# Expert layers of a transformer: TensorE's order fixed to blocks of full and half columns, the norm's output transposed back instead of added by identity matmuls

## The chip, the cores and the metric

The kernel runs on one core of a Trainium2 chip. The metric is the device time of one execution in microseconds (us). TensorE does the matmuls and transposes, VectorE (DVE), ScalarE (ACT) and GpSimd (POOL) work elementwise, and SyncE (SP) issues the DMAs that bring the weights from HBM. [...]

## The reference, cut to what matters

256 tokens of 1024 features go through a block with two feed-forward parts and a mixer, then through two further layers, each with a mixer of its own, a norm, a mixture of experts and a gated embedding, and a second norm. The change touches the expert part of these two layers:

```python
x = layer_norm(DEEPNORM_ALPHA * x + mix, ln_mix_g[i], ln_mix_b[i])
ple = (p[i] @ ple_w_proj[i]) * jax.nn.sigmoid(x @ ple_w_gate[i])
ffn = grouped_moe(x, router_w, router_bias, moe_w1[i], moe_w3[i], moe_w2[i])
x = layer_norm(DEEPNORM_ALPHA * x + ffn + ple, ln_ffn_g[i], ln_ffn_b[i])

def grouped_moe(x, router_w, router_bias, w1, w3, w2):   # 16 experts, two per token
    ...                                                  # gates: (tokens, 16)
    h = jax.nn.silu(jnp.einsum('td,edf->etf', xt, w1)) * jnp.einsum('td,edf->etf', xt, w3)
    h = h * gates.T[:, :, None].astype(h.dtype)          # w1, w3: 1024 x 512 per expert
    y = jnp.einsum('etf,efd->td', h, w2)                 # w2: 512 x 1024 per expert
```

## The kernel before

**Tiling.** `moe_layer` works on pairs of experts, p = 0 to 7. The router gives each expert up to 64 slots for its tokens. Three kinds of step follow for each pair. *Gather*: one-hot matrices `oh` pull the tokens' features (in two parts, `nh` and `nl`) into slots, `xgp<-oh,nh` and `xgp<-oh,nl`, 256 columns each, for two pairs at once: 32 matmuls at p = 0, 2 and 4 (and ahead of the loop). *Up* (`up`): `h1` and `h3` are 16 program matmuls each, with 64 slots as the stationary columns. Expert e=0 writes rows 0 to 63 of the PSUM tile and e=1 rows 64 to 127, so each matmul uses one half of the array's columns and the two experts alternate. *Down* (`down`): the product `es` of silu(h1) and h3 is transposed in four pieces (`hidden_T`, `ehT`, copied to `ehTs`), and 16 more half-column program matmuls give `ey`. These half-column operands are plain fp32, and the trace holds two records for each program matmul, so `h` shows 64 records a pair and `ey` 32.

**Combine.** `ey` is scaled and split into two fp32r parts `yh` (ScalarE) and `yl` (VectorE), and `combine` adds them into the tokens with eight full-column matmuls by the transposed one-hots `ohT` (made in `slots_T` from `ohTp`). For p = 0 to 2 they go to PSUM tiles `early` that VectorE adds into `x` (tile `acc`); from p = 3 (`last`) they accumulate in four PSUM banks `comb`. Two more things are added into `comb` by matmuls with the identity: 32 of `xTh` and `xTl`, the norm's output held transposed (128 features by 256 tokens, two parts), at the end of p = 3, and eight of `acch` and `accl`, the two parts of `x`, at the end of p = 6. The gate of the embedding, `gacc`, is 96 full-column matmuls during p = 1 to 3 and holds the same four banks before `comb`. The end of the layer reads `comb` for the norm's statistics (`bst`).

**The branch.** At p = 4 the kernel reads a flag (`ci`): if an expert got more than 64 tokens, the rest is computed by `overflow`. In the runs shown the branch jumps over it. Every engine has its own copy of the branch, L1400, and of the join behind it.

**What sets the order.** Python emits instructions in program order and a scheduler then orders each engine's list by dependences, priorities and its own cost figures. `after(i, j)` adds a pure order between two instructions. In the expert loop nothing but data, buffers and the branch fixes TensorE's order. The weights come through a ring of tiles of 512 KB (`Stream`, `W.next`); SP issues each load when the tile's last reader is done, in the fixed order of the list of loads. `mm` (L342) and `mm3` (L337) are the helpers that issue nearly all matmuls, so their lines, L343 and L338 to L340, name many different things in the profile; tiles' names tell them apart.

Of the kernel before, what the change touches and what calls it, by code (L numbers as in the profile page):

```python
# [15 lines left out]
P = 128  # L16
# [33 lines left out]
def transformer_kernel(ctx: ExitStack, tc: tile.TileContext, A, out, stop=None):  # L50
# [67 lines left out]
    def fb(ap):  # L118
        return ap.bitcast(F32)
# [211 lines left out]
    def split_to(hi, lo, src, scale=1.0):  # L331
# [2 lines left out]
            return V.tensor_tensor(lo, src, fb(hi), op=OP.subtract)  # L334
        return V.scalar_tensor_tensor(lo, src, scale, fb(hi), op0=OP.mult, op1=OP.subtract)  # L335

    def mm3(o, lh, ll, rh, rl, start, stop):  # L337
        PE.matmul(o, lh, rh, start=start, stop=False)  # L338
        PE.matmul(o, lh, rl, start=False, stop=False)  # L339
        PE.matmul(o, ll, rh, start=False, stop=stop)  # L340
# [746 lines left out]
    def layer_norm_T(x, before, row, eps, then=None):  # L1087

        qs, hi, lo = [[], []], [], []

        def allocate():
            hi.extend(H([4, T], F32R, "xTh") for _ in range(2))
            lo.extend(H([4, T], F32R, "xTl") for _ in range(2))

        def split(i):
            tk = slice(i * P, (i + 1) * P)
            for kk in range(2):
                split_to(hi[kk][:, :, tk], lo[kk][:, :, tk], qs[i][kk])

        def chunks():  # L1100
            return ([hi[k // 4][:, k % 4, :] for k in range(8)], [lo[k // 4][:, k % 4, :] for k in range(8)])

        def later():
            allocate()
            split(0)
            split(1)
            return chunks()
# [125 lines left out]
    def slots_T(oh, sc, p):  # L1233

        t_ = PT([T + NE], name="ohTp")
        for t in range(2):
            PE.transpose(t_[:, t * P:(t + 1) * P], fb(oh[p // 2])[:, t, p % 2 * P:(p % 2 + 1) * P], ident)  # L1237
# [30 lines left out]
    def moe_layer(i, x, before, row, eps, next_gains):  # L1268
# [75 lines left out]
        def hidden_T(s):  # L1344
            ht = PT([4, P], name="ehT")
            for f in range(4):
                PE.transpose(ht[:, f, :], s[:, f * P:(f + 1) * P], ident)  # L1347
            hT = Q([4, P], name="ehTs")
            S.copy(hT, ht)  # L1349
            return hT  # L1350

        def down(p, hT, sg):
            ys = [PT([512], name="ey") for _ in range(2)]
            for f in range(4):
                ws = [W.next() for _ in range(2)]
# [4 lines left out]
            y = [(Q([512], F32R, "yh"), Q([512], F32R, "yl")) for _ in range(2)]  # L1360
            for j in range(2):
                split_to(*y[j], ys[j], sg)
            return y

        def combine(p, y, o):

            skip = dict(skip_group_check=True) if p >= last else {}
            for t in range(2):
                o_ = o[:, t * P:(t + 1) * P]
                cs = [PT([512], name="early") for _ in range(2)] if p < last else comb[t]  # L1370
                for j in range(2):
                    mm(cs[j], o_, y[j][0], start=p <= last, stop=False, **skip)
                for j in range(2):
                    mm(cs[j], o_, y[j][1], start=False, stop=p < last or p == 7, **skip)
                    if p < last:
                        d = slice(j * 512, (j + 1) * 512)
                        if p == 0:
                            V.tensor_copy(x[t][:, d], cs[j])
                        else:
                            V.tensor_tensor(x[t][:, d], x[t][:, d], cs[j], op=OP.add)  # L1380

        last = len(PLE) - 3
        acc = [[PA([512], name="gacc") for _ in range(2)] for _ in range(2)]

        def gate(k):
            wh, wl = wsplit(G)
            for t in range(2):
                for j in range(2):
                    c = slice(j * 512, (j + 1) * 512)
                    tk = slice(t * P, (t + 1) * P)  # L1390
                    mm3(acc[t][j], xTh[k][:, tk], xTl[k][:, tk], wh[:, 0, c], wl[:, 0, c], k == 0, k == 7)

        h1, h3 = PT([512], name="h1"), PT([512], name="h3")
        up(0, h1)
        up(0, h3)
        s = hidden(h1, h3)
        for p in range(8):
            if p == 4:
                v = nc.values_load(ci[0:1, 0:1], min_val=0, max_val=T)
                with tc.If(v > CAP):  # L1400
                    overflow(i, x, nh, nl, late, row)
            if p < 7:
                h1 = PT([512], name="h1")
                up(p + 1, h1, (0, 1))
            hT = hidden_T(s)
            if p < 7:
                up(p + 1, h1, (2, 3))
            o, sg = slots_T(oh, sc, p)
            if p == 7:
                gains(*next_gains, W.loads[W.pos + 7])  # L1410
            y = down(p, hT, sg)
            if p == 0:
                xTh, xTl = xT()
            if p <= last:
                for k in range(*PLE[p + 1:p + 3]):
                    gate(k)
            if p == last:
                for t in range(2):
                    for j in range(2):
                        c = slice(j * 512, (j + 1) * 512)  # L1420
                        g = Q([512], name="pg")
                        S.activation(g, acc[t][j], AF.Sigmoid)
                        V.tensor_tensor(g, g, pro[t][:, c], op=OP.mult)
                        V.tensor_tensor(x[t][:, c], x[t][:, c], g, op=OP.add)
                comb = [[PA([512], name="comb") for _ in range(2)] for _ in range(2)]
            if p < 7:
                h3 = PT([512], name="h3")
                up(p + 1, h3)
                s = hidden(h1, h3)
                if p % 2 == 0 and p < 6:  # L1430
                    oh.append(onehot(rk, p // 2 + 1))
                    gather(p // 2 + 1, oh)
            if p == 0:

                x[:] = [H([D], name="acc") for _ in range(2)]
            combine(p, y, o)
            if p == last:
                for t in range(2):
# [5 lines left out]
            if p == 6:  # L1444
                for t in range(2):
                    xs = XH([D], F32R, "acch"), X([D], F32R, "accl")
                    split_to(*xs, x[t])
                    for part in xs:
                        for j in range(2):
                            mm(comb[t][j], identr, part[:, j * 512:(j + 1) * 512], start=False, stop=False,  # L1450
                               skip_group_check=True)
        return lambda t: comb[t]

    def overflow(i, x, nh, nl, late, row):
# [248 lines left out]
```

## Time and profile before

| | us |
|---|---|
| median of 3 executions (lowest to highest) | 1340.33 (1338.78 to 1343.26) |
| the profiled execution, its own time | 1343.85 |
| its span in the trace | 1342.2 |
| PE busy / DVE busy / ACT busy / POOL busy | 1281.4 / 600.3 / 514.1 / 266.2 |
| layer 0's experts: to the branch, round the branch, behind it | 145.59, 29.14, 86.13 |
| layer 1's experts: the same three, and the tail to the end | 144.49, 28.33, 86.20, 14.33 |

The span is the time from the first to the last instruction of the profiled execution; its own time also has what lies around it. A stage in the table is a stretch of the trace: "to the branch" starts with the first pair's `h`, "round the branch" starts where pair 4's last `h` ends, "behind it" ends with the last `ey`. In a row of the timeline, the first number is the start in us from the span's start, the second the length up to the end of the last instruction in the row, and `x8` means eight instructions of this kind in a row on that engine. Matmuls overlap in the pipeline, so the pace of TensorE is the distance from one start to the next, and not the length. [...] The DMA share counts the core's 16 DMA engines, and can come out a little over 1.

### The profile page before, as it was taken

To read this page: it belongs to the slowest core of one execution; us is meant where nothing else is said; L and a number is where in the kernel's file an instruction comes from. 1 tells how busy PE (TensorE), PEld (TensorE's weight loads), DVE (VectorE), ACT (ScalarE), POOL (GpSimd) and SP (SyncE) were. 2 spreads that over 40 slices of the span, in tenths; PEclk is the share of its full clock that TensorE was granted. 3 is DMA by queue.
4 is the path that set the end of the run, shared out by engine and by line. 5 is a ranking of instruction groups with operands and counts; after the bars stand their busy time and mean duration, and the time that the engine had idled before them with its cause. 6 is when DMAs were issued, how large, how long until landed. Compare 5 with 4: busy or idle time off the path is not lost. (4 is left out here: it accounts for less than half of the span.)

```text
span 1342.2 us, 19692 instructions
## 1 busy us (share of the span) xinstructions
PE 1281.4 (95%) x7758; PEld 913.1 (68%) x7758; DVE 600.3 (45%) x959; ACT 514.1 (38%) x774; POOL 266.2 (20%) x318
## 2 busy tenths in 40 slices
PE   8999999999998999989999999997999999999996
PEld 7999987877897999878444554334988635454432
DVE  6554458786665455586241221107555522121113
ACT  5444445575444544435221131104676421131110
POOL 4000010003699273240011020004021110220001
PEclk9999999999998999999989998997999999998998
DMA  9666656444453556559789999998535698999991
GB/s 341 219 186 187 189 158 203 128 156 142 150 180 126 157 174 197 187 174 336 275 317 370 394 342 342 385 382 285 186 109 193 236 383 319 381 344 357 366 402 38
DMA packets 175277, 335.41 MB, mean 250 GB/s; under 512 B 10338, under 2 KB 72306, under 8 KB 175171
## 3 DMA queue, kind: packets, MB, share of 16 engines
q1 hardware_dynamic: 173696, 330.34, 70.2%
q0 software_dynamic: 896, 2.98, 0.6%
q8 instruction: 66, 1.08, 0.3%
q10 hardware_dynamic: 578, 0.67, 0.2%
q14 instruction: 41, 0.33, 0.1%
HBM read 332.91 MB, written 1.05 MB: 249 GB/s over the span
## 5 line engine op out<-in xcount | busy, mean ns | idle before, releaser
L316 DVE TENSOR_TENSOR wlo<-w,whi 128x1024 fp32r<-128x1024 f32 x200 | 256.9, 1289 | 215.4 <-ACT whi L301 210.5
L301 ACT ACTIVATE whi<-w 128x1024 fp32r<-128x1024 f32 x234 | 246.4, 1059 | 268.4 <-PE hT L339 119.7
L343 PE MATMUL h<-w,xg 128*64 128x512 f32 x1024 | 254.4, 607 | 0.0
L338 PE MATMUL hT<-xTh,whi 128*128 128x256 f32 x704 | 201.7, 287 | 0.1
L339 PE MATMUL hT<-xTl,whi 128*128 128x256 f32 x704 | 201.1, 286 | 0.3 <-DVE xTl L334 0.2
L340 PE MATMUL hT<-xTh,wlo 128*128 128x256 f32 x704 | 200.5, 285 | 0.0
L343 PEld LDWEIGHTS h<-w,xg 128*64 128x64 f32 x1024 | 73.4, 139 | 137.8 <-issue 129.3
L339 PEld LDWEIGHTS hT<-xTl,whi 128*128 128x128 f32 x704 | 136.9, 195 | 1.4 <-DVE xTl L334 0.8
L338 PEld LDWEIGHTS hT<-xTh,whi 128*128 128x128 f32 x704 | 136.9, 194 | 1.3 <-ACT xTh L332 0.5
L340 PEld LDWEIGHTS hT<-xTh,wlo 128*128 128x128 f32 x704 | 136.7, 194 | 0.0
L343 PE MATMUL ey<-w,ehTs 128*64 128x512 f32 x512 | 115.1, 595 | 0.2
L316 POOL TENSOR_TENSOR wlo<-w,whi 128x1024 fp32r<-128x1024 f32 x16 | 38.0, 2399 | 242.6 <-ACT whi L301 242.6
L343 PEld LDWEIGHTS ey<-w,ehTs 128*64 128x64 f32 x512 | 38.2, 137 | 65.1 <-issue 60.0
L335 DVE SCALAR_TENSOR_TENSOR yl<-ey,sgate,yh 128x512 fp32r<-128x512 f32 x32 | 23.6, 749 | 124.2 <-ACT yh L332 123.4
L338 PE MATMUL tr<-xTh,whi 128*128 128x256 f32 x256 | 73.9, 289 | 0.4 <-ACT xTh L332 0.4
L339 PE MATMUL tr<-xTl,whi 128*128 128x256 f32 x256 | 73.2, 286 | 0.3 <-DVE xTl L334 0.3
L340 PE MATMUL tr<-xTh,wlo 128*128 128x256 f32 x256 | 72.6, 284 | 0.0
L1341 DVE TENSOR_TENSOR es<-es,h 128x512 f32<-128x512 f32 x16 | 11.0, 687 | 129.7 <-PE h L343 116.3
L338 PE MATMUL yacc<-whi,hh 128*128 128x512 f32 x176 | 68.8, 391 | 0.0
L339 PE MATMUL yacc<-wlo,hh 128*128 128x512 f32 x176 | 68.7, 390 | 0.0
L340 PE MATMUL yacc<-whi,hl 128*128 128x512 f32 x176 | 68.6, 390 | 0.0
L350 POOL TENSOR_TENSOR brs<-rp,cm 128x1 f32<-128x1 f32 x8 | 4.4, 550 | 312.4 <-DVE rp L349 312.4
(444 smaller groups left out, 2180.3 us busy)
## 6 DMA issues: line engine op xcount, KB each, us to landing
w<-in_moe_w SPq DMA_DIRECT2D x384, 512.0 KB, 8.3
w<-in_ffn_w SPq DMA_DIRECT2D x132, 512.0 KB, 4.4
w<-in_w_in SPq DMA_DIRECT2D x28, 512.0 KB, 4.3
w<-in_sb_qkv SPq DMA_DIRECT2D x24, 512.0 KB, 10.3
w<-in_ple_gate SPq DMA_DIRECT2D x16, 512.0 KB, 7.9
w<-in_w_out SPq DMA_DIRECT2D x8, 512.0 KB, 3.3
w<-in_ab_w_in SPq DMA_DIRECT2D x8, 512.0 KB, 4.5
w<-in_ab_w_out SPq DMA_DIRECT2D x8, 512.0 KB, 4.0
```

The lines of the kernel that those rows point to most:

```text
L301: a = S.activation(hi, t, AF.Copy)
L316: i = eng.tensor_tensor(lo, t, fb(hi), op=OP.subtract)
L335: return V.scalar_tensor_tensor(lo, src, scale, fb(hi), op0=OP.mult, op1=OP.subtract)
L338: PE.matmul(o, lh, rh, start=start, stop=False)
L339: PE.matmul(o, lh, rl, start=False, stop=False)
L340: PE.matmul(o, ll, rh, start=False, stop=stop)
L343: PE.matmul(o, l, r, start=start, stop=stop, **kw)
L350: cur["pow"] = G.tensor_tensor(o, t, cm05[:, :n], op=OP.pow)
L1341: V.tensor_tensor(s, s, h3, op=OP.mult)
```

## The change

Five things are edited, all in the expert layers.

1. A helper `pinned` gives each matmul and transpose of the loop an `after` on the one before it, so TensorE's order is the order of emission. The chain is cut at the branch.
2. The emission is rewritten. For each pair: the gather (now at odd p, ahead of the pairs that need it), `combine` of the pair before, `hidden_T`, `slots_T`, then `up` of the next pair for `h1`, `down`, the gate, and `up` of the next pair for `h3`.
3. The 32 identity matmuls on `xTh` and `xTl` go. `residual`, behind the branch at p = 4, makes `yT = xTh + xTl` on VectorE (four adds of 128x512), transposes it back on TensorE (16 of 128x128, into PSUM tiles `yn`) and adds it to `x` on VectorE (four adds).
4. The eight identity matmuls of `acch` and `accl` (`collect`) move from the end of p = 6 to ahead of p = 7's transposes; `combine` goes half by half of the features.
5. For p = 7, `down` takes its eight weight tiles at once, finishes the first 512 features (all four f), splits them, and then does the other 512.

```diff
+    def pinned(i):
+        if "pin" in cur:
+            if cur["pin"] is not None:
+                after(i, cur["pin"])
+            cur["pin"] = i
...
     def mm(o, l, r, start=True, stop=True, **kw):
-        PE.matmul(o, l, r, start=start, stop=stop, **kw)
+        pinned(PE.matmul(o, l, r, start=start, stop=stop, **kw))
...
         def down(p, hT, sg):
...
+            if p < 7:
+                for f in range(4):
+                    ws = [W.next() for _ in range(2)]
+                    for j in range(2):
+                        part(f, j, ws)
                 for j in range(2):
-                    for e in range(2):
-                        mm(ys[j][e * 64:(e + 1) * 64, :], hT[:, f, e * 64:(e + 1) * 64],
-                           ws[e][:, 0, j * 512:(j + 1) * 512], start=f == 0, stop=f == 3)
...
+            else:
+                wf = [[W.next() for _ in range(2)] for _ in range(4)]
+                for j in range(2):
+                    for f in range(4):
+                        part(f, j, wf[f])
+                    split_to(*y[j], ys[j], sg)
...
+        def residual():
+            for kk in range(2):
+                yT = [Q([2, T], name="yT") for _ in range(2)]
+                for n in range(2):
+                    c = slice(2 * n, 2 * n + 2)
+                    V.tensor_tensor(yT[n], fb(whole_h[kk])[:, c], fb(whole_l[kk])[:, c], op=OP.add)
+                for t in range(2):
+                    pn = PT([4, P], name="yn")
+                    for k in range(4):
+                        pinned(PE.transpose(pn[:, k, :], yT[k // 2][:, k % 2, t * P:(t + 1) * P], ident))
+                    d = slice(kk * 512, (kk + 1) * 512)
+                    V.tensor_tensor(x[t][:, d], x[t][:, d], pn.rearrange("p a b -> p (a b)"), op=OP.add)
...
         for p in range(8):
             if p == 4:
+                del cur["pin"]
                 v = nc.values_load(ci[0:1, 0:1], min_val=0, max_val=T)
                 with tc.If(v > CAP):
                     overflow(i, x, nh, nl, late, row)
-            if p < 7:
+                cur["pin"] = None
+            if p == 0:
                 h1 = PT([512], name="h1")
-                up(p + 1, h1, (0, 1))
+                up(1, h1)
+            if p % 2 and p < 7:
+                oh.append(onehot(rk, (p + 1) // 2))
+                gather((p + 1) // 2, oh)
...
+            if p == last + 1:
+                residual()
+                comb = [[PA([512], name="comb") for _ in range(2)] for _ in range(2)]
+            if p > 0:
+                combine(p - 1, y, o)
+            if p == 7:
+                collect()
             hT = hidden_T(s)
-            if p < 7:
-                up(p + 1, h1, (2, 3))
             o, sg = slots_T(oh, sc, p)
+            if 0 < p < 7:
+                h1 = PT([512], name="h1")
+                up(p + 1, h1)
...
-            if p == last:
-                for t in range(2):
-                    tk = slice(t * P, (t + 1) * P)
-                    for k in range(8):
-                        for t_ in (xTh, xTl):
-                            mm(comb[t][k // 4][:, k % 4 * P:(k % 4 + 1) * P], t_[k][:, tk], identr,
-                               start=False, stop=False, skip_group_check=True)
```

TensorE's list in layer 0 behind pair 4's `ey`, before: `h` is the up step of pair 5 and `xgp` the gather for pairs 6 and 7.

```order
L343 MATMUL comb<-yh,ohT 128x512
L343 MATMUL xgp<-oh,nh 128x256
L343 MATMUL xgp<-oh,nl 128x256
L343 MATMUL h_9829<-w_7683,xg 64x512
L343 MATMUL xgp<-oh,nh 128x256
L343 MATMUL xgp<-oh,nl 128x256
L343 MATMUL xgp<-oh,nh 128x256
L343 MATMUL xgp<-oh,nl 128x256
L343 MATMUL xgp<-oh,nh 128x256
L343 MATMUL xgp<-oh,nl 128x256
L343 MATMUL h_9829<-w_7689,xg 64x512
```

The same `h` of pair 5 in the list after, where it joins pair 4's `ey`:

```order
L350 MATMUL ey<-w_7634,ehTs 64x512
L350 MATMUL ey<-w_7669,ehTs 64x512
L350 MATMUL ey<-w_7634,ehTs 64x512
L350 MATMUL ey<-w_7669,ehTs 64x512
L350 MATMUL h_9829<-w_7671,xg 64x512
L350 MATMUL h_9829<-w_7677,xg 64x512
L350 MATMUL h_9829<-w_7671,xg 64x512
L350 MATMUL h_9829<-w_7677,xg 64x512
```

The gather no longer stands between the matmuls of `h`; all 32 of it follow behind the sixteenth.

TensorE's list in layer 0 at the join behind the branch, before:

```order
L1400 UNCONDITIONAL_BRANCH x2
L343 MATMUL comb<-yh,ohT 128x512 x2
L343 MATMUL comb<-yl,ohT 128x512 x2
L343 MATMUL comb<-identr,xTh 128x128
L343 MATMUL comb<-identr,xTl 128x128
```

And after:

```order
L1460 UNCONDITIONAL_BRANCH x2
L1436 MATMUL yn<-identr,yT 128x128 x16
L350 MATMUL comb<-yh,ohT 128x512
L350 MATMUL comb<-yl,ohT 128x512
L350 MATMUL comb<-yh,ohT 128x512
L350 MATMUL comb<-yl,ohT 128x512
```

Sixteen transposes stand first, ahead of the eight `comb` of pair 3, half of which stood ahead of the branch.

VectorE's list at the same place after, with the new adds around the branch (its rows between the branch and the join, which are skipped, are left out):

```order
L1432 TENSOR_TENSOR yT<-xTh,xTl 128x512 x2
L1348 TENSOR_TENSOR es<-es,h_7668 128x512
L1459 TENSOR_LOAD ci
L1460 COMPARE_AND_BRANCH
```

```order
L1460 UNCONDITIONAL_BRANCH x2
L1438 TENSOR_TENSOR acc<-acc,yn 128x512 x2
L1432 TENSOR_TENSOR yT<-xTh,xTl 128x512 x2
L1438 TENSOR_TENSOR acc<-acc,yn 128x512 x2
L334 TENSOR_TENSOR accl<-acc,acch 128x1024 x2
```

Two of the four `yT` adds stand ahead of the branch, the other two behind the first pair of adds to `acc`.

## Rows read from the trace of the kernel before

**Rows 1.** Busy time by stage: A, B, C of layer 0, then of layer 1, tail

```profile
core 0: us, PE busy (x) PEld busy (x) DVE busy (x) ACT busy (x) POOL busy (x), PEclk, DMA share, GB/s
650.85:796.44 145.59, 142.92 (x673) 67.54 (x672) 35.40 (x58) 33.26 (x49) 19.02 (x8) 0.98 0.94 350
796.44:825.58 29.14, 26.20 (x116) 14.03 (x116) 3.36 (x5) 3.58 (x5) 0.00 (x0) 0.82 0.90 329
825.58:911.71 86.13, 84.31 (x352) 32.69 (x348) 10.25 (x21) 9.99 (x19) 0.00 (x0) 1.00 1.04 385
...
1068.85:1213.34 144.49, 141.82 (x673) 66.39 (x672) 35.40 (x58) 33.25 (x49) 19.03 (x8) 0.99 0.95 357
1213.34:1241.67 28.33, 26.23 (x116) 13.81 (x116) 3.36 (x5) 3.58 (x5) 0.00 (x0) 0.82 0.95 347
1241.67:1327.87 86.20, 84.38 (x352) 32.67 (x348) 10.26 (x21) 9.98 (x19) 0.00 (x0) 1.00 0.79 301
1327.87:1342.20 14.33, 2.40 (x10) 1.35 (x8) 9.52 (x18) 2.29 (x4) 3.69 (x6) 0.73 0.19 73
```

**Rows 2.** Timeline of TensorE in A, pair 1: start, length, what

```profile
702.36 0.66 PE L1347 MATMUL ehT<-identr,es 128*128 128x128 f32 x4
702.94 3.65 PE L343 MATMUL h<-w,xg 128*64 128x512 f32 x16
706.53 0.44 PE L1237 MATMUL ohTp<-identr,oh 128*128 128x128 f32 x2
...
707.25 7.09 PE L343 MATMUL ey<-w,ehTs 128*64 128x512 f32 x32
714.27 0.50 PE L339 MATMUL gacc<-wlo,xTh 128*128 128x512 f32 x1
714.61 0.40 PE L340 MATMUL gacc<-whi,xTl 128*128 128x512 f32 x1
714.84 0.39 PE L338 MATMUL gacc<-whi,xTh 128*128 128x512 f32 x1
```

**Rows 3.** Timeline of TensorE in layer 0's C, mixed kinds

```profile
828.18 1.07 PE L343 MATMUL h<-w,xg 128*64 128x512 f32 x2
829.18 0.39 PE L343 MATMUL xgp<-oh,nh 128*128 128x256 f32 x1
...
830.09 1.93 PE L343 MATMUL h<-w,xg 128*64 128x512 f32 x6
831.95 0.39 PE L343 MATMUL xgp<-oh,nh 128*128 128x256 f32 x1
...
897.53 1.07 PE L343 MATMUL h<-w,xg 128*64 128x512 f32 x2
```

**Rows 4.** Timeline of TensorE in layer 0's C: its two waits, in brackets

```profile
887.34 0.74 PE L343 MATMUL comb<-yh,ohT 128*128 128x512 f32 x2 [0.81 <-ACT yh L332]
...
903.47 0.66 PE L1347 MATMUL ehT<-identr,es 128*128 128x128 f32 x4 [0.85 <-DVE es L1341]
```

**Rows 5.** Branch and join, both layers (ns min/median/max, first and last start), then layer 0's timeline

```profile
L1400 PEldq COMPARE_BRANCH  x2: 6227/6544/6862, 793.6 to 1210.3; - x2
...
L1400 DVEq EVENT_SEMAPHORE  x2: 21/21/21, 803.1 to 1220.1; - x2
...
796.75 0.69 DVE L1341 TENSOR_TENSOR es<-es,h 128x512 f32<-128x512 f32 x1 [3.55 <-PE h L343]
...
800.68 0.70 PE L343 MATMUL comb<-yh,ohT 128*128 128x512 f32 x2 [2.94 <-PEq L1400]
```

**Rows 6.** Half clock: two identity matmuls of layer 0, and a stretch of layer 1

```profile
806.18 0.41 PE L343 MATMUL comb<-identr,xTl 128*128 128x128 f32 x1
806.40 0.41 PE L343 MATMUL comb<-identr,xTh 128*128 128x128 f32 x1
...
1218.40:1228.60 10.20, 10.20 (x40) 6.95 (x40) 2.36 (x2) 2.00 (x2) 0.00 (x0) 0.50 0.88 323
```

**Rows 7.** Stretches at the end of the weight stream, columns as in rows 1

```profile
1305.00:1310.00 5.00, 5.00 (x17) 1.84 (x16) 0.00 (x0) 0.00 (x0) 0.00 (x0) 1.00 0.84 334
1310.00:1320.00 10.00, 9.15 (x34) 3.28 (x34) 0.69 (x1) 0.00 (x0) 0.00 (x0) 1.00 0.01 2
```

More of the change, by code (lines that the diff above doesn't have):

```diff
@@ L335, in split_to @@
         return V.scalar_tensor_tensor(lo, src, scale, fb(hi), op0=OP.mult, op1=OP.subtract)
+    def pinned(i):
[3 more added lines that the diff above has]
+            cur["pin"] = i
     def mm3(o, lh, ll, rh, rl, start, stop):
-        PE.matmul(o, lh, rh, start=start, stop=False)
-        PE.matmul(o, lh, rl, start=False, stop=False)
-        PE.matmul(o, ll, rh, start=False, stop=stop)
+        pinned(PE.matmul(o, lh, rh, start=start, stop=False))
+        pinned(PE.matmul(o, lh, rl, start=False, stop=False))
+        pinned(PE.matmul(o, ll, rh, start=False, stop=stop))
     def mm(o, l, r, start=True, stop=True, **kw):
-        PE.matmul(o, l, r, start=start, stop=stop, **kw)
+        pinned(PE.matmul(o, l, r, start=start, stop=stop, **kw))
     def rpow(o, i, eps):
@@ L1106, in later @@
             split(1)
-            return chunks()
+            return chunks(), (hi, lo)
         if not then:
@@ L1236, in slots_T @@
         for t in range(2):
-            PE.transpose(t_[:, t * P:(t + 1) * P], fb(oh[p // 2])[:, t, p % 2 * P:(p % 2 + 1) * P], ident)
+            pinned(PE.transpose(t_[:, t * P:(t + 1) * P], fb(oh[p // 2])[:, t, p % 2 * P:(p % 2 + 1) * P], ident))
         for t in range(2):
@@ L1346, in hidden_T @@
             for f in range(4):
-                PE.transpose(ht[:, f, :], s[:, f * P:(f + 1) * P], ident)
+                pinned(PE.transpose(ht[:, f, :], s[:, f * P:(f + 1) * P], ident))
             hT = Q([4, P], name="ehTs")
@@ L1353, in down, with part @@
             ys = [PT([512], name="ey") for _ in range(2)]
-            for f in range(4):
-                ws = [W.next() for _ in range(2)]
-                for j in range(2):
-                    for e in range(2):
-                        mm(ys[j][e * 64:(e + 1) * 64, :], hT[:, f, e * 64:(e + 1) * 64],
-                           ws[e][:, 0, j * 512:(j + 1) * 512], start=f == 0, stop=f == 3)
-            y = [(Q([512], F32R, "yh"), Q([512], F32R, "yl")) for _ in range(2)]
-            for j in range(2):
-                split_to(*y[j], ys[j], sg)
+            y = [(Q([512], F32R, "yh"), Q([512], F32R, "yl")) for _ in range(2)]
+            def part(f, j, ws):
+                for e in range(2):
+                    mm(ys[j][e * 64:(e + 1) * 64, :], hT[:, f, e * 64:(e + 1) * 64],
+                       ws[e][:, 0, j * 512:(j + 1) * 512], start=f == 0, stop=f == 3)
+            if p < 7:
[3 more added lines that the diff above has]
+                        part(f, j, ws)
+                for j in range(2):
+                    split_to(*y[j], ys[j], sg)
[4 more added lines that the diff above has]
+                        part(f, j, wf[f])
+                    split_to(*y[j], ys[j], sg)
             return y
         def combine(p, y, o):
-            skip = dict(skip_group_check=True) if p >= last else {}
-            for t in range(2):
[L1369 to L1375, printed above, removed]
+            if p < last:
+                for t in range(2):
+                    cs = [PT([512], name="early") for _ in range(2)]
+                    for n in range(2):
+                        for j in range(2):
+                            mm(cs[j], o[:, t * P:(t + 1) * P], y[j][n], start=n == 0, stop=n == 1)
+                    for j in range(2):
                         d = slice(j * 512, (j + 1) * 512)
@@ L1380, in combine @@
                             V.tensor_tensor(x[t][:, d], x[t][:, d], cs[j], op=OP.add)
+            else:
+                for j, t in ((j, t) for j in range(2) for t in range(2)):
+                    for n in range(2):
+                        mm(comb[t][j], o[:, t * P:(t + 1) * P], y[j][n], start=p == last and n == 0,
+                           stop=p == 7 and n == 1, skip_group_check=True)
         last = len(PLE) - 3
@@ L1391, in gate, with embedding, collect @@
                     mm3(acc[t][j], xTh[k][:, tk], xTl[k][:, tk], wh[:, 0, c], wl[:, 0, c], k == 0, k == 7)
+        def embedding():
+            for t in range(2):
+                for j in range(2):
+                    c = slice(j * 512, (j + 1) * 512)
+                    g = Q([512], name="pg")
+                    S.activation(g, acc[t][j], AF.Sigmoid)
+                    V.tensor_tensor(g, g, pro[t][:, c], op=OP.mult)
+                    V.tensor_tensor(x[t][:, c], x[t][:, c], g, op=OP.add)
+        def residual():
+            for kk in range(2):
+                yT = [Q([2, T], name="yT") for _ in range(2)]
+                for n in range(2):
+                    c = slice(2 * n, 2 * n + 2)
+                    V.tensor_tensor(yT[n], fb(whole_h[kk])[:, c], fb(whole_l[kk])[:, c], op=OP.add)
+                for t in range(2):
+                    pn = PT([4, P], name="yn")
[3 more added lines that the diff above has]
+                    V.tensor_tensor(x[t][:, d], x[t][:, d], pn.rearrange("p a b -> p (a b)"), op=OP.add)
+        def collect():
+            for t in range(2):
+                xs = XH([D], F32R, "acch"), X([D], F32R, "accl")
+                split_to(*xs, x[t])
+                for part in xs:
+                    for j in range(2):
+                        mm(comb[t][j], identr, part[:, j * 512:(j + 1) * 512], start=False, stop=False,
+                           skip_group_check=True)
+        cur["pin"] = None
         h1, h3 = PT([512], name="h1"), PT([512], name="h3")
@@ L1417, in moe_layer @@
             if p == last:
[L1418 to L1425, printed above, removed]
+                embedding()
             if p < 7:
@@ L1429, in moe_layer @@
                 s = hidden(h1, h3)
[L1430 to L1436, printed above, removed]
-            if p == last:
-                for t in range(2):
-                    tk = slice(t * P, (t + 1) * P)
-                    for k in range(8):
-                        for t_ in (xTh, xTl):
-                            mm(comb[t][k // 4][:, k % 4 * P:(k % 4 + 1) * P], t_[k][:, tk], identr,
-                               start=False, stop=False, skip_group_check=True)
[L1444 to L1451, printed above, removed]
+        combine(7, y, o)
+        del cur["pin"]
         return lambda t: comb[t]
```

6 lines of the change are left out of this document (5 added, 1 removed).

## Prediction

> **What bounds the kernel now.** First I cut the profiled execution (1343.85 us, 3.5 us above the median of the runs shown) into stages of the two expert layers and read busy time, TensorE's granted clock and DMA share for each [rows 1]. Per layer: A is pairs 0 to 3, B the flag and the branch, C the rest of the matmuls, and in layer 1 a tail. In A and C TensorE is busy for nearly all of the stage (84.31 of 86.13 us in C); VectorE and ScalarE are idle most of it. So TensorE's own pace sets these stages, and the weights come second: in layer 0's C the DMA share is 1.04. In B TensorE has a hole and runs at a clock of 0.82.
>
> Busy is not pace, so next I read TensorE in order of time. `h` and `ey` use half the columns, expert e=0 in one half and e=1 in the other; nearly all else uses all 128. From two starts [rows 2]: 16 records of `h` take 706.53-702.94 = 3.59 us, 32 of `ey` 714.27-707.25 = 7.02 us. So a further half record costs 3.43/16 = 0.2144 us, and a visit to the halves a fixed 0.16 us. On the other side four 128-column transposes take 702.94-702.36 = 0.58 us where 0.11 us apiece, as below at half clock halved [rows 6], would be 0.44; and the first 512-column matmul after a change takes 0.34 us to the next start, the one behind it 0.23. So the full side pays some 0.11 to 0.15 us as well, and a round trip between the kinds costs 0.27 to 0.31 us.
>
> Then C, where the scheduler mixes the two kinds [rows 3]. `h x2` lasts 1.00 us to the next start (829.18-828.18), `h x6` 1.86 us. By the figures above they should take 0.59 and 1.45. Each lacks a partner: it holds an odd number of program matmuls (two records each), so one half runs alone, and each pays 0.41 us. Two waits stand there too [rows 4]: 0.81 us on `yh`, 0.85 us on `es`.
>
> **The change, part by part (per layer).**
>
> *C, the order.* Counted in TensorE's records from 825.58 to 911.71 us: 22 visits to the halves, of them 17 unpaired: 8 `h x2` and 7 `h x6`, the first at 828.18 and the last at 897.53 [rows 3], and two longer ones. The fixed order has four, each with both halves. Unpaired: 17 x 0.41 = 7.0. Visits: 18 x 0.31 = 5.6 (4.9 at 0.27). The waits: `es` is now covered by a `comb` block of eight, 8 x 0.23 = 1.8 us, against a wait that starts when `h` ends; `yh` is covered by the 16 matmuls of `h` behind `ey`, 6.9 us. Both go, 1.66. Together 14.3. A second way: 258 half records x 0.2144 = 55.3, 4 visits 0.6, 32 `comb` at 0.23 = 7.4, 32 gather matmuls at 0.12 (six between two visits take 830.09-829.18 = 0.91 us [rows 3]; less 0.2 of entry) 3.8, three `ehT` and `ohTp` blocks at about 1.15 make 3.5, four entries 0.6: 71.2, so 14.9 less than 86.13. I take **14.5**, with 12.5 to 16 as ends: the lower if half the round-trip cost stays, the upper from the second way with shorter transposes.
>
> *A, the order.* Pairs 1 to 3 visit the halves four times each before and twice now, pair 0 once less: 7 round trips x 0.31 = 2.2; pair 0's `ey` now stands right behind `ohTp`, which costs about 0.2 for the copy of `ehT`. **2.0**, ends 1.0 and 2.3.
>
> *B, branch and residual.* The 32 identity matmuls go. They run at half clock, 0.22 us apart [rows 6], so 7 us. In comes the chain DVE `yT`, PE `yn`, DVE add. What it costs lies in the join. After the flag is read, TensorE is back soonest: its branch lasts 6.2 to 6.9 us, but starts ahead of its queue, so its gap in the trace is 2.94 us (matmuls resume at 800.68). VectorE is back only at 803.1 (1220.1 in layer 1) [rows 5], since its branch waits for `es`, an add at 796.75. Before, TensorE's first work after the branch (`comb`) needs nothing from VectorE; the adds came from PSUM accumulation. Now the first work is `yn`, and the order of waits shows it tied to VectorE's count behind the join, so TensorE idles from the end of `h`, 796.5, to 803.1, and behind it stand `comb`, `ehT`, `ohTp` and all of `h`; nothing may pass, since the order is pinned. From there, at half clock: four transposes 0.9; two adds and two `yT` at 0.69 [rows 5] 2.8 to 3.0, the second half of `yn` 0.9 (807.7); `comb` 8 x 0.46 = 3.7 (811.4); `ehT` and `ohTp` 1.2 to 1.9 (813); 64 half records 13.9 (826.9). Before, that point was 825.58. Loss 1.3; in layer 1 the same 6.7 us from `h` to the join stand against a B that is 0.8 shorter, so 2.1. [...] Ends: +1 (clock soon full) and -5 (half clock through `h`, and a second wait of `ehT` for a PSUM buffer).
>
> [...]
>
> *Tail.* For p=7 `down` finishes one half of the output first, so half of the last split and of `comb` can start while `ey` still runs. But VectorE's order is now `yl`, statistics, `yl`, statistics, so the second `yl` waits behind one statistics step that needs `comb`. **+0.2**, ends -0.4 and +0.6.
>
> *Moved weights.* The DMA order is the same. But p=7's eight tiles are all needed within the first half of `ey`, 16 x 0.2144 = 3.4 us earlier. In layer 1 the stream ends at about 1309.2 (share 0.84 in 1305 to 1310, 0.01 behind it [rows 7]), while the last `ey` ends near 1327.9: the last tile lies ready some 17.8 us, so 14.4 with the earlier need. A, B and C together come 14.1 to 14.9 sooner. The shortfall is about zero, and a tile of 0.5 MB takes 1.36 us at the 385 GB/s of C, so I take **-0.7**, ends 0 and -6.
>
> *Sum.* Layer 0: 2.0-1.6+14.5+0.2-0.7 = 14.4. Layer 1: 13.6. Together 28.0: the profiled execution would be 1315.9, the median 1340.33-28.0 = **1312.3 us**.
>
> **The rivals.**
>
> *The weights become the bound (0.15).* C has 64 tiles of four records each, 64 x 1.36 = 87 us at the measured rate, against 71.5 us of matmuls; only the lead of the ring (14.4 us) pays the difference. If slots come free later than I reckon (B is longer, and a slot is freed by its matmul), 3 to 6 us per layer are given back in the last pairs: about 1321. For it: share 1.04 in C. Against: in layer 1 the share is 0.79 over C, since nothing follows.
>
> [...]
>
> *The join costs more (0.13).* Pinned behind `yn`, TensorE waits for VectorE twice and half clock reaches into `h` and `ey`: -5 more per layer, 1322. Decides if TensorE restarts after 806.
>
> *The pairing does not come back (0.04).* Were the 0.41 us due to something other than the missing partner (the change of weights' tile, say), 14 us of the gain are missing: 1326. Against: 16 and 32 in a row keep 0.2144.
>
> *Slower (0.04).* A pinned order turns a late operand into an idle TensorE instead of other work. A hole of 2.94 us is followed by 10.2 us of half clock [rows 5, 6], so each costs 2 + 5.1 = 7 us; holes of 0.8 us left the clock at 1.00 [rows 1, 4]. The place would be the seven joins `comb` to `ehT` in each layer. It decides from four such holes, 28 us; with six it is 1354. Against: each join has 1.8 us of cover, and the wait without it was 0.85.
>
> **How the numbers follow.** The forecast, with 0.64, gives **1312.3**. Its own ends are about 1303 (C 16, B 0, no wait for weights) and 1321. The rivals at 1321 and 1322 lie at the edge, so the range 1303 to 1323 leaves out the slower rival, the pairing one and the far ends of the rest, some 0.17. A difference of 0.3%, 4 us, is about what a measurement can tell from no change. Faster by more: all but the slower rival and a little of the weights, 0.94. Within: 0.02. Slower: 0.04.
>
> **What would show it.** In the changed profile: in C no `h x2`, blocks of 64 half records at about 13.9 us, C near 71.5 us (wrong above 75). B of 30 to 31 us with TensorE restarting when VectorE does; wrong if `yn` starts with TensorE's own return. In the last pairs, TensorE waiting for DMA at `h` or `ey`: none, or under 2 us in all. A shorter by 2 us. If C comes at 71.5 and the time above 1318, B or the weights are the mis-sized term; if C stays above 80, the pairing is.

## The result, and the profile after

The changed kernel takes **1309.51 us** (median of four executions, 1307.48 to 1309.66) against 1339.55 us for the kernel before (1337.27 to 1343.26): 0.9764 of its time, 95% interval 0.9746 to 0.9782, or 30.0 us less. The forecast was 1312.3 us with a gain of 28.0, range 1303 to 1323. The profiled execution took 1309.66 us, its span is 1308.0; the one before was 3.5 us above its median, so the two spans differ by 34.2 us, some four more than the medians.

The stages of [rows 1] in the profile after (PEclk is the clock granted to TensorE, as a share of full speed); each line starts and ends at the same instructions as its counterpart (A ends with pair 4's `h`, C 0.2 us before the end of the last `ey`, with 352 matmul records as before):

```profile
core 0: us, PE busy (x) PEld busy (x) DVE busy (x) ACT busy (x) POOL busy (x), PEclk, DMA share, GB/s
649.99:792.00 142.01, 138.84 (x673) 65.80 (x672) 36.63 (x60) 33.20 (x49) 18.93 (x8) 1.00 0.96 356
792.00:822.47 30.47, 22.32 (x101) 11.52 (x100) 7.32 (x11) 3.56 (x5) 0.00 (x0) 0.83 0.85 310
822.47:894.70 72.23, 71.65 (x352) 31.46 (x348) 11.10 (x22) 12.71 (x22) 0.00 (x0) 1.00 1.04 395
...
1050.42:1193.83 143.41, 140.27 (x673) 67.28 (x672) 36.62 (x60) 33.11 (x49) 18.93 (x8) 0.99 0.95 355
1193.83:1223.00 29.17, 21.35 (x101) 10.87 (x100) 7.32 (x11) 3.57 (x5) 0.00 (x0) 0.82 0.89 326
1223.00:1293.85 70.85, 70.75 (x352) 32.05 (x348) 11.11 (x22) 10.73 (x20) 0.00 (x0) 1.00 0.99 377
1293.85:1308.00 14.15, 2.52 (x9) 1.34 (x8) 8.81 (x17) 1.71 (x3) 3.70 (x6) 0.69 0.20 74
```

Against [rows 1], C fell from 86.13 to 72.23 and from 86.20 to 70.85 us with the same work in it. A fell by 3.6 and 1.1 us. B grew by 1.3 and 0.8 us, and the tail fell by 0.2. So the gain is C's, and the branch cost a little. The stages make 31.9 of the 34.2 us between the spans; the rest lies outside them.

What C looks like now, TensorE in order of time, answers [rows 3]:

```profile
832.77 0.28 PE L350 MATMUL xgp<-oh,nl 128*128 128x256 f32 x1
...
833.38 0.40 PE L350 MATMUL comb<-yh,ohT 128*128 128x512 f32 x1
...
835.22 0.60 PE L1354 MATMUL ehT<-identr,es 128*128 128x128 f32 x4
...
836.32 7.09 PE L350 MATMUL h<-w,xg 128*64 128x512 f32 x32
843.24 7.04 PE L350 MATMUL ey<-w,ehTs 128*64 128x512 f32 x32
850.11 7.04 PE L350 MATMUL h<-w,xg 128*64 128x512 f32 x32
857.07 0.50 PE L350 MATMUL comb<-yh,ohT 128*128 128x512 f32 x1
```

There is no `h x2` or `h x6` left: 96 half records take 857.07-836.32 = 20.75 us, 0.2161 apiece with the step back to full columns at the end in it. Neither `comb` nor `ehT` has a wait in brackets; those of [rows 4] are gone.

The branch and the join of layer 0, answering [rows 5]:

```profile
L1460 PEldq EVENT_SEMAPHORE  x2: 51/51/51, 794.4 to 1196.3; - x2
L1460 DVEq EVENT_SEMAPHORE  x2: 21/21/21, 798.7 to 1200.2; - x2
...
798.84 1.94 PE L1436 MATMUL yn<-identr,yT 128*128 128x128 f32 x8 [6.68 <-DVEq L1460]
802.25 2.06 PE L1436 MATMUL yn<-identr,yT 128*128 128x128 f32 x8 [1.47 <-DVE yT L1432]
803.96 0.78 PE L350 MATMUL comb<-yh,ohT 128*128 128x512 f32 x1
...
799.00:808.00 9.00, 7.53 (x28) 6.03 (x28) 6.31 (x8) 2.00 (x2) 0.00 (x0) 0.52 0.94 342
```

TensorE is back from its branch at 794.4 and stands there until VectorE is back at 798.7: 6.68 us idle, then 1.47 more for the second `yT`. The last line is a stretch of 9 us behind it at a granted clock of 0.52, about half.

And the weights at the end of layer 0, TensorE's loads of stationary operands:

```profile
889.11 0.19 PEld L350 LDWEIGHTS ey<-w,ehTs 128*64 128x64 f32 x2 [1.12 <-DMA w<-in_moe_w]
890.42 0.20 PEld L350 LDWEIGHTS ey<-w,ehTs 128*64 128x64 f32 x4 [1.12 <-DMA w<-in_moe_w]
```

Twice pair 7's `ey` waits 1.12 us for a tile, where the pause between two loads is otherwise 0.29: 1.7 us lost. The whole step takes 8.93 us to the next start, against 7.09 where pair 7 keeps the plain order (an experiment below), so 1.8. In layer 1 it takes 7.53 against 7.10, 0.4 more, with one wait for a tile, of 0.32 us.

### The profile page after: what moved, and what is told of

Same layout as the page of the kernel before. It is cut to its first block, busy times and chain, and to the rows that moved or that the text cites. A ratio compares the mean times of both kernels' runs of the same rounds, so it can differ in the third digit from the quotient of the medians.

```text
span 1308.0 us, 19650 instructions
## 1 busy us (share of the span) xinstructions
PE 1240.8 (95%) x7726; PEld 903.6 (69%) x7726; DVE 613.1 (47%) x975; ACT 514.6 (39%) x774; POOL 269.5 (21%) x318
## 5 line engine op out<-in xcount | busy, mean ns | idle before, releaser
L316 DVE TENSOR_TENSOR wlo<-w,whi 128x1024 fp32r<-128x1024 f32 x200 | 266.0, 1336 | 209.3 <-ACT whi L301 206.9
L350 PE MATMUL h<-w,xg 128*64 128x512 f32 x1024 | 225.5, 594 | 0.5
L332 ACT ACTIVATE yh<-ey,sgate 128x512 fp32r<-128x512 f32 x32 | 22.0, 688 | 168.7 <-PE ey L350 128.3
```

Source lines behind the costliest of these rows:

```text
L316: i = eng.tensor_tensor(lo, t, fb(hi), op=OP.subtract)
L332: cur["act"] = S.activation(hi, src, AF.Copy if isinstance(scale, float) else AF.Identity, scale=scale)
L350: pinned(PE.matmul(o, l, r, start=start, stop=stop, **kw))
```

## The experiments

Every kernel was measured against the kernel before on the same chip. Twelve ran, on four chips, where the medians of the kernel before lie between 1339.5 and 1341.2 us; a difference between two kernels from different chips is good to that much at best.

**Which part carries the gain: the pin alone.** The old emission, chained:

```diff
     def mm(o, l, r, start=True, stop=True, **kw):
-        PE.matmul(o, l, r, start=start, stop=stop, **kw)
+        pinned(PE.matmul(o, l, r, start=start, stop=stop, **kw))
```

(and the same in `mm3`, `hidden_T` and `slots_T`; nothing else of the change).

> The kernel before with only TensorE's order pinned to its own, old emission: identity matmuls, old places of the gather and of p=7 kept. Theory (the gain is the pairing of the halves and the two waits): C of layer 0 falls from 86.1 to about 73.5 us (17 unpaired x 0.41, 14 visits fewer at 0.2 to 0.31, waits 1.66), B stays at 28 to 29 us since nothing behind the join needs VectorE, A as before; no wait for weights; in all about 1315 us. Rival (the gain needs the new blocks): C stays above 80 us and the time above 1325. Rival (the residual on VectorE is worth something): it stays more than 8 us behind the changed kernel's 1309.5.

Measured: 1308.5 us, ratio 0.977 (0.974 to 0.9801). Its B and C of layer 0:

```profile
793.76:822.36 28.60, 26.16 (x117) 14.42 (x117) 3.36 (x5) 3.58 (x5) 0.00 (x0) 0.82 0.96 358
822.36:893.88 71.52, 71.42 (x352) 30.66 (x348) 10.35 (x21) 10.64 (x20) 0.00 (x0) 1.00 1.04 395
```

C falls to 71.5 us, 2.0 below the theory, with the old emission and 8 visits to the halves. Pinning alone gives the whole gain; the new blocks, the residual and pair 7's halves together add nothing to it that these runs could tell.

**The blocks without the pin.**

```diff
     def pinned(i):
-        if "pin" in cur:
-            if cur["pin"] is not None:
-                after(i, cur["pin"])
-            cur["pin"] = i
+        return i
```

> The changed kernel without the pinning: the new emission, but the scheduler may move TensorE's instructions; it mixes h and comb in C again. Theory: some 15 unpaired visits per layer come back, so C is at 84 to 87 us, B at 30 us, and the time near the kernel before, 1336 to 1341 us. Rival (the blocks or the residual carry the gain without the pin): under 1325 us.

Measured: 1340.84 us, ratio 1.0005 (0.9989 to 1.0021). TensorE in its C:

```profile
819.30 0.73 PE L347 MATMUL comb<-yh,ohT 128*128 128x512 f32 x2 [0.76 <-ACT yh L332]
819.96 1.07 PE L347 MATMUL h<-w,xg 128*64 128x512 f32 x2
820.96 0.73 PE L347 MATMUL comb<-yl,ohT 128*128 128x512 f32 x2
...
826.53 1.93 PE L347 MATMUL h<-w,xg 128*64 128x512 f32 x6
828.39 0.39 PE L347 MATMUL xgp<-oh,nh 128*128 128x256 f32 x1
```

The scheduler mixes the kinds again, with the same 1.00 and 1.86 us and a wait for `yh`, and the gain is gone. As expected.

**Is it the partner?** Expert 0's eight matmuls, then expert 1's, in `h3` of pairs 5 to 7:

```diff
-                up(p + 1, h3)
+                up(p + 1, h3, solo=p >= 4)
...
+            if solo:
+                wa = [[W.next() for _ in range(2)] for _ in range(4)]
+                for e in range(2):
+                    for k in range(8):
```

> The changed kernel, but the up step of h3 for pairs 5 to 7 does all eight matmuls of expert 0 and then all eight of expert 1, so that no half has a partner beside it; blocks, visits, data and work stay. Theory (the 0.41 us in C was the missing partner): 32 records go from 0.2144 to about 0.42 us each, 6.6 us a block, six blocks, 39.5 us, less 2.5 us of waits for weights that vanish: about 1346 us, slower than the kernel before. Rival (the cost was the change between the kinds of columns or of weight tiles): within 5 us of 1309.5.

Measured: 1343.05 us, ratio 1.002 (1.0008 to 1.0032), 33.5 us over the changed kernel, or 31.9 when each is taken from the kernel before on its own chip. One such block:

```profile
824.85 12.24 PE L350 MATMUL h<-w,xg 128*64 128x512 f32 x32
837.02 0.39 PE L350 MATMUL xgp<-oh,nh 128*128 128x256 f32 x1
```

12.17 us to the next start instead of 6.97. Six blocks make 31.2 us. A record alone takes (12.17-0.1)/32 = 0.38 us and not the 0.42 I had from `h x2`. The order of the experts within one kind of column, with no visit added, loses what the change gains: the partner is shown. The edit also makes neighbours add into the same rows of PSUM. No run takes the two apart, but `comb` and `gacc` add into one tile in a row too and stay 0.23 us apart (they are fp32r, `h` is plain fp32).

**What a visit costs.** `ehT` and `ohTp` back between the halves of `h` for pairs 1 to 6, with pair 7 in plain order:

```diff
-            hT = hidden_T(s)
-            o, sg = slots_T(oh, sc, p)
             if 0 < p < 7:
                 h1 = PT([512], name="h1")
-                up(p + 1, h1)
+                up(p + 1, h1, (0, 1))
+            hT = hidden_T(s)
+            if 0 < p < 7:
+                up(p + 1, h1, (2, 3))
+            o, sg = slots_T(oh, sc, p)
```

> The changed kernel with pair 7's down in plain order (1306.6 us) and, for pairs 1 to 6, the transposes ehT and ohTp put back between the halves of h: two more visits a pair, 24 in all, each with both partners. By the price of the prediction (0.31 us) 7.4 us more, 1314; by what the run with the old emission and a pinned order shows (0.25 us) 6.0 us, 1312.6; if visits with partners cost nothing, 1306.6.

Measured: 1313.99 us, ratio 0.98 (0.9774 to 0.9825), 7.4 over its own base of 1306.57: 0.31 us a visit. The two ran on different chips; when each is taken from the kernel before on its own chip, 6.2 us are left, 0.26 a visit. One such pair in the trace:

```profile
836.33 0.40 PE L350 MATMUL comb<-yh,ohT 128*128 128x512 f32 x1
...
838.27 3.65 PE L350 MATMUL h<-w,xg 128*64 128x512 f32 x16
841.85 0.66 PE L1354 MATMUL ehT<-identr,es 128*128 128x128 f32 x4
842.44 3.65 PE L350 MATMUL h<-w,xg 128*64 128x512 f32 x16
846.02 0.44 PE L1244 MATMUL ohTp<-identr,oh 128*128 128x128 f32 x2
...
846.74 7.09 PE L350 MATMUL ey<-w,ehTs 128*64 128x512 f32 x32
```

846.74-836.33 = 10.41 us from the first `comb` to `ey`, where the changed kernel needs 843.24-833.38 = 9.86 for the same work: 0.55 for two visits, 0.27 each.

**Pair 7 in plain order.** `if p < 7` becomes `if p < 8` in `down`:

> The changed kernel with pair 7's down in the same order as the other pairs, so that its last tiles are needed 3.4 us later. Theory (the weights bind the end of the layers): the waits for DMA in pair 7's ey go (1.9 us in layer 0, about 0.6 in layer 1), the ends lose about 0.4 each, so about 1308 us. Rival (the early half is worth more than the waits): 1310 to 1311 us.

Measured: 1306.57 us, ratio 0.975 (0.9724 to 0.9776), 2.9 less than the changed kernel. Pair 7's `ey` shows no wait for DMA any more. The early half was worth less than the early need of the tiles cost: in layer 1, from the end of the last `ey` to the end of the span, the plain order takes 13.56 us and the halves take 13.96. The two intervals overlap; the waits that go are in the trace.

**The residual, four ways.** First the identity matmuls in its place, behind `comb`:

```diff
-            if p == last + 1:
-                residual()
...
+            if p == last + 1:
+                for t in range(2):
+                    tk = slice(t * P, (t + 1) * P)
+                    for k in range(8):
+                        for t_ in (xTh, xTl):
+                            mm(comb[t][k // 4][:, k % 4 * P:(k % 4 + 1) * P], t_[k][:, tk], identr, ...)
```

> The changed kernel with the 32 identity matmuls behind comb of pair 3 in place of the transposes and VectorE's adds. Theory (the join with VectorE eats what the fewer matmuls save): TensorE restarts about 4 us after the end of h instead of 6.7, then comb 2.4, identity 7.0, so B at 28.5 to 29 us against 30.4 and 29.1, and since the last weights hold the end of layer 0, the time stays within 2 us of 1309.5. Rival (the residual saves): 4 us or more slower, 1313.5.

Measured: 1302.3 us, ratio 0.973 (0.9685 to 0.9774), 7.2 less. I had expected a tie. B of both layers, and TensorE at layer 1's join:

```profile
793.54:821.60 28.06, 24.02 (x116) 12.56 (x116) 3.36 (x5) 3.57 (x5) 0.00 (x0) 0.88 0.95 346
1192.73:1215.28 22.55, 20.63 (x117) 10.80 (x116) 3.27 (x5) 3.41 (x5) 0.00 (x0) 1.00 1.04 389
...
1195.85 0.47 PE L350 MATMUL comb<-yh,ohT 128*128 128x512 f32 x1 [1.92 <-PEq L1460]
```

TensorE waits only for its own branch, 1.92 us instead of 6.3, and in layer 1 the granted clock stayed at 1.00, so the identity matmuls ran at full pace. That is 6.6 us off layer 1's B alone. The expectation had half clock in both layers, and layer 0's B, 28.06 us, came out near it. So much of the gain hangs on the clock that layer 1 kept, and one of the four executions took 1310.68 us.

With pair 7 in plain order as well:

> The changed kernel with the identity matmuls in place of the residual on VectorE (1302.3 us alone) and pair 7's down in plain order. Theory (weights bind the ends): the waits for weights in pairs 6 and 7, 1.5 us in layer 0 and 2.0 in layer 1, mostly go: 1299 to 1300 us. Rival (each layer's end is set elsewhere): 1302 us or more.

Measured: 1300.89 us, ratio 0.9698 (0.9673 to 0.9722). Only 1.4 less than with the halves, which the intervals can't tell from nothing, and the waits moved more than they went: in layer 1 pair 6's last `h` now waits for tiles, and its block takes 9.20 us in place of 6.97 (`PEld h` on DMA, 3.4 us in six waits, the longest 1.1). With B that much shorter, 22.53 us, the weights do bind layer 1.

Then the residual kept, but behind the eight `comb`, pair 7 plain:

```diff
-            if p == last + 1:
-                residual()
...
                 combine(p - 1, y, o)
+            if p == last + 1:
+                residual()
```

> The changed kernel with pair 7's down in plain order (1306.6 us) and the eight comb of pair 3 ahead of the residual's transposes at the branch. Theory (the residual's place behind the join costs, because it waits for VectorE there): the comb fill part of the hole, the transposes start when VectorE is back, as before, so B gains only the 2.7 to 3.5 us of comb that stood behind them: 1300 to 1303 us if both layers gain it, never below the late residual's 1301.1 by more than noise. Rival (any order of comb and transposes is the same): 1306 us.

Measured: 1300.52 us, ratio 0.9715 (0.969 to 0.974), 6.0 below the same kernel with the residual first. Its B of both layers:

```profile
791.65:818.09 26.44, 21.25 (x101) 11.13 (x100) 7.50 (x11) 3.48 (x5) 0.00 (x0) 0.87 0.98 363
1186.52:1213.24 26.72, 22.79 (x100) 11.99 (x100) 7.50 (x11) 3.47 (x5) 0.00 (x0) 0.81 0.97 357
```

Against 30.47 and 29.17: 4.0 and 2.5 us, about the `comb` that no longer stand behind the wait.

The residual moved away from the branch, behind `comb` of pair 5, pair 7 plain (`if p == 5: residual()`):

> The changed kernel with pair 7's down in plain order and the residual moved behind comb in pair 5: transposes and VectorE's adds as in the change, but with yT long done and nothing near the branch. Theory (the residual itself is cheaper than the identity matmuls; what it cost was its place at the join): B falls to 19 to 25 us, C gains about 1.9 for the sixteen transposes, no wait for yT or for VectorE behind the branch. By TensorE's path 1294 to 1297 us; if the weights bind as in the run with identity matmuls and plain down, 1299 to 1301. Rival (the residual costs wherever it stands): 1305 us or more.

Measured: 1301.12 us, ratio 0.9709 (0.9692 to 0.9727). B is 24.44 and 24.47 us, but with two holes a layer, of 2.1 to 2.3 us for TensorE's branch and 1.7 to 2.1 at `ehT`, which waits for VectorE's join once nothing else stands there. So the theory held on the place, and the time is the upper of my two, though not for the reason I gave: no wait for weights longer than 0.3 us, the usual pause between two loads, is in its last pairs. It, the run before it and the identity matmuls with pair 7 plain end within 0.6 us of each other, so whether the residual is cheaper than the identity matmuls in themselves is not shown.

And the residual ahead of the branch, pair 7 plain (`if p == last: residual()` at the end of the pair):

> The changed kernel with pair 7's down in plain order (1306.6 us) and the residual ahead of the branch, at the end of pair 3, so that nothing behind the join waits for VectorE. Theory (the join with VectorE is what the residual costs): TensorE no longer waits 6.7 us for VectorE behind the branch; B falls from 30.4 and 29.1 us to 25 to 28, and the time to about 1300 us, where the weights begin to bind. Rival (VectorE's adds, or half clock, cost it wherever they stand): 1305 to 1307 us.

Measured: 1308.12 us, ratio 0.9766 (0.9743 to 0.979). The theory fell. The join of layer 0:

```profile
794.14 1.39 PE L1436 MATMUL yn<-identr,yT 128*128 128x128 f32 x8
...
802.43 1.09 PE L1354 MATMUL ehT<-identr,es 128*128 128x128 f32 x4 [6.91 <-DVEq L1460]
...
L1460 PEldq COMPARE_BRANCH  x2: 6182/6412/6642, 795.3 to 1196.6; - x2
```

The transposes ahead of the branch wait for `yT`, so TensorE's sequencer reaches the branch only at 795.3, when its queue is all but empty, and then the branch lies bare: a hole of 6.5 us in layer 1, and of 6.91 in layer 0, where VectorE's return came last. In the changed kernel it got there at 788.3, 3.7 us ahead of the end of `h`. Here a wait just ahead of the branch costs as much as one just behind it. Layer 0 has a hole of 3.45 us more within `ohTp` that the profile puts to no releaser; what that is stays open.

**Do the weights bind the late residual?** In pairs 4 to 6 both experts use the first expert's tiles of w2, so part of the computation is changed:

```diff
-                for e in (2 * p, 2 * p + 1):
+                for e in (2 * p, 2 * p + 1)[:1 if 4 <= p < 7 else 2]:
                     specs.append(rows(A["moe_w2"][i, e], k * P, 1, 0, 1024))
```

> The kernel of the late residual with less to load: in pairs 4 to 6 both experts use the first expert's tiles of w2, so 12 of 208 tiles per layer are left out (about 16 us of the weights' stream), while TensorE does the same matmuls. If the weights bind the end of each layer in the late-residual kernel, TensorE's waits for DMA vanish and the time falls by 2 to 5 us against it; if not, both are equal within 1 us.

Measured: 1301.44 us, ratio 0.9711 (0.9694 to 0.9728): equal. In the late-residual kernel the weights don't bind, and my reason for expecting 1299 to 1301 there was wrong.

**The one-hots a pair earlier.** On top of the late residual, the one-hots of pairs 2 and 3 are made a pair earlier, ahead of `yl` on VectorE:

```diff
             o, sg = slots_T(oh, sc, p)
+            if p == 0:
+                oh.append(onehot(rk, 1))
```

> The late-residual kernel (1301.1 us) with the one-hots for pairs 2 and 3 made a pair earlier, ahead of VectorE's yl, so that the gather at pair 1 needn't wait for them. Theory (with no wait for weights left, TensorE's path still sets the layers): the waits of 0.75 and 1.9 us per layer go, with them about 1.7 us of half clock, so 5 to 9 us in all: 1292 to 1296 us. Rival (the weights' stream binds now): above 1299 us, with waits for DMA in pairs 6 and 7.

Measured: **1290.4 us** (1287.98 to 1291.76), ratio 0.963 (0.9614 to 0.9646), 10.7 less than without, and below my 1292 to 1296. A of both layers:

```profile
649.00:788.02 139.02, 138.49 (x673) 65.70 (x672) 33.34 (x58) 33.05 (x49) 19.41 (x8) 1.00 0.97 364
1036.69:1175.68 138.99, 138.47 (x673) 65.74 (x672) 33.34 (x58) 33.07 (x49) 19.42 (x8) 1.00 0.98 367
```

A was 143.4 us in both layers of its base, where the gather stalled 2.7 us for `oh` and the mean granted clock of A was 0.99, against 1.00 here. 4.4 us a layer are the 2.7 us of waits and 1.7 more, which I had expected from half clock. They make 8.8 of the 10.7; B, 23.33 and 23.93 us, makes 1.7 more, which I had not expected. The two profiled executions lie 13.5 us apart, more than the medians, and the rest is not traced.

## Why the prediction was right, and where it was off

- **C, right in mechanism and close in size.** Forecast -14.5 each and -0.7 for weights; measured -13.9 and -15.3 with the weights' waits in them, some -15.7 in both layers without. The partner is shown by the solo block, the order by the two runs with pin or blocks alone. The price of a lone record was a little high (0.38, not 0.42), that of a visit is 0.27, the lower end of the 0.27 to 0.31 I had. At 0.27 a visit and 2 x (0.38-0.2144) = 0.33 for a lone pair of records the first way of adding comes to about 12, so it leaves out some 3 us that C did gain, and what they are stays open; the second way, which adds up what remains, came within 1 us.
- **A, mis-sized.** Forecast -2.0; layer 1 shows -1.1. Where nothing waits, the visits give what they should: in pair 2 of layer 1 the old order takes 1154.12-1143.60 = 10.52 us from the first `early` to `ey`, the new one 1134.82-1124.84 = 9.98, again 0.27 a visit. In pair 3 it is 10.55 against 10.44 only, since there, as in pair 1, `h` now stands right behind `ohTp` and waits for the copy of `ehT`, which the sum had for pair 0 alone. Pair 2 before and after, then the wait in pair 3:

```profile
1143.60 0.73 PE L343 MATMUL early<-yh,ohT 128*128 128x512 f32 x2
...
1154.12 7.09 PE L343 MATMUL ey<-w,ehTs 128*64 128x512 f32 x32
...
1124.84 0.73 PE L350 MATMUL early<-yh,ohT 128*128 128x512 f32 x2
...
1134.82 7.04 PE L350 MATMUL ey<-w,ehTs 128*64 128x512 f32 x32
...
1164.64 0.20 PEld L350 LDWEIGHTS h<-w,xg 128*64 128x64 f32 x4 [0.24 <-ACT ehTs L1356]
```

- **A in layer 0.** The -3.6 has another cause: the gather at pair 1 ran faster than before, 6.10 us against 8.72, at a clock that stayed higher (A as a whole 1.00 against 0.98), while in layer 1 it took 7.57 and 7.58. So this is a difference between executions and not one that the change is known to make.
- **B, right.** Forecast +1.6 and +2.4; measured +1.3 and +0.8. TensorE restarted with VectorE's return, after 6.68 us in layer 0 and 6.35 in layer 1. The 1.6 and 2.4 are the 1.3 and 2.1 read off the rows and 0.3 more for half clock that lasts into `h`. No run read here shows that 0.3: in the changed kernel 32 records of the first `h` behind it took 6.92 us in both layers, the full pace. In layer 1 half clock (0.50 granted from 1200 to 1206.8) ended at about 1207, when the starts of `comb` went from 0.43 to 0.23 us apart, so half of them ran at full pace.
- **What the sum left out:** I priced B against the kernel before, where the clock was down too. Against a pinned order with the same work placed elsewhere, or done by identity matmuls, the residual's place costs 5.5 to 6 us (1306.6 against 1301.1, 1300.5 and 1300.9). The change brings 30 us, though its best part alone brings 31.5, within the error of the two.
- **The weights, the first rival, in small.** 1.8 us in layer 0 and 0.4 in layer 1, against 0.7 forecast for each; the forecast read the lead of the weights from layer 1, and layer 0 paid. Pair 7's early half is what made them. On TensorE alone the mixed order cost about 15 us a layer (1340.8 against 1309.5 us over two), against 1.8 us of waits at the end of one layer for the blocks with pair 7's early half.
- **The other rivals.** No pinned join of `comb` and `ehT` shows a wait, so the slower case had no place to start. Its price was read across layers: the hole of 2.94 us is layer 0's, and the 10.2 us of half clock are layer 1's, behind a hole of 2.10. The pairing did come back. The join cost no more than forecast.
- **The tail, right.** Forecast -0.2, ends +0.4 and -0.6; measured 14.15 against 14.33 us in layer 1, and in layer 0 5.75 against 5.97 up to the next `xTp`. Both effects that the prediction named are there: the wait of `comb` for `yh`, 0.81 us before, is gone, and the second `yl`, behind a statistics step, holds `comb` for 0.75.

## What to carry to other kernels

Where matmuls use half of the array's columns, look at the order of single instructions: neighbours on opposite halves ran side by side here (0.2144 us a record, 0.38 alone), and a scheduler can put something between them, which shows as odd numbers of records in a row and not as idle time. An order pinned by hand is worth as much as the gaps it leaves: put instructions that need nothing from another engine next to a branch, on both sides of it, and keep the waits away from there (5.5 to 6 us here). After a gain, look for the stall that was hidden: here one-hots a pair too late were worth 10 us more.

## What the runs showed of the hardware

A jumped branch lasted 6.0 to 6.9 us on TensorE in the five traces where its length was read (the kernel before, the changed one, the two with identity matmuls behind `comb`, the one with the residual ahead of the branch), but what it cost went with how early the sequencer reached it. In the changed kernel, with `h` queued for another 3.7 us it was back 2.4 us after the end of `h`; with a queue all but empty, in the run with the residual ahead of the branch, the hole was 6.5 us.

A hole of about 2 us was followed by half clock (0.50 granted) in some places here and not in others. In the two runs with identity matmuls behind `comb`, layer 1 stayed at 1.00 behind holes of 1.92 and about 1.9 us; the kernel before fell to 0.50 behind one of 2.10. In layer 0 of the first of these runs the matmuls kept full pace behind a hole of 2.25 us and lost it after a second one of 1.79 us, for which the profile has no releaser (granted 1.00 from 790 to 800 us, 0.66 from 800 to 810). What this is worth shows in the second run, within one execution: the same instructions took 29.22 us in layer 0's B, at 0.77 behind a hole of 2.43 us, and 22.53 in layer 1's, at 1.00. I had taken half clock behind the branch as given. The join of layer 1 in the kernel before, then B of both layers in the second run:

```profile
1216.74 0.70 PE L343 MATMUL comb<-yh,ohT 128*128 128x512 f32 x2 [2.10 <-PEq L1400]
...
795.06:824.28 29.22, 26.79 (x116) 15.77 (x116) 3.36 (x5) 3.58 (x5) 0.00 (x0) 0.77 0.89 327
1192.34:1214.87 22.53, 20.63 (x116) 10.80 (x116) 3.27 (x5) 3.36 (x5) 0.00 (x0) 1.00 1.05 389
```

Part of the spread of 3 to 8 us between executions of one kernel may be this. The slowest of the four executions with identity matmuls and pair 7 in halves, 1310.68 us, has the lowest mean granted clock, 0.967 against 0.976 to 0.978; that the clock is the whole of it is not shown.
